# High halves of the transposed rows ahead of the low ones, one step of the first FFN pair later, token sums of the output parts some steps later

## The chip, the core and the metric

The kernel runs on one core of one Trainium2 chip. A core has a matrix engine (TensorE, in the profile PE, with its weight loads as PEld), two elementwise engines (VectorE = DVE and ScalarE = ACT), GpSimd (POOL), and queues for transfers between the chip's memory and the core (SyncE = SP issues most of them). The metric is the device time of one execution in microseconds; lower is better. Times in tables are medians of several runs. The profile comes from one further execution, with every instruction's start and duration.

## The reference

One layer of an encoder block, for 256 tokens of width 2048, all in float32. Three token mixers (dilated windows, grouped attention, attention to memory tokens) are merged by gates, projected and added to the input; then comes a gated feed-forward net (FFN) of inner width 5632. The change touches what stands from the projection on:

```python
merged = gates[:, :, 0] * (oa @ w_br_a) + gates[:, :, 1] * (ob @ w_br_b) + gates[:, :, 2] * (oc @ w_br_c)
x = x + merged @ w_o
hf = rms_norm(x, g_ffn) @ w_ffn_in
x = x + (silu(hf[..., :D_FF]) * hf[..., D_FF:]) @ w_ffn_out
```

## The kernel before

Every product of float32 matrices is made of three matmuls in a faster format (fp32r): each operand is split into a high half (the rounded value) and a low half (what is left), and high x high, high x low and low x high are summed in PSUM. ACT writes the high halves of a weight block (`whi`, in `halves`, line L397) and DVE the low ones (`wlo`, in `low`, L407). Both take from a ring of four buffers, and every fifth from a buffer of its own, so the `whi` of a step gets the buffer of the one five steps before, and must wait until PE has done that step's last matmul.

Work goes in pairs of output columns (`pair`), each 512 wide for 256 tokens in two halves (t = 0, 1); a pair runs a list of steps. A step reads weights, makes their halves and issues matmuls of a 128x128 stationary block against 512 columns:

- `dN`, `DN`: block N of the inner dimension, whole, for the first or the second column of the pair (12 matmuls each, into the sums Y, V or Z, Q).
- `fN`, `gN`, `hN`, `pN`, `qN`: block N by a scheme of seven products instead of eight (the scheme of Strassen and Winograd). `fN` needs both columns' weights (two loads and an adding load by POOL, in `fetch_both`), `gN` their sums (L506, L507, and L513 or L529 on DVE), `h`, `p` and `q` what is left of them. These steps also need sums of the token rows, which `token_sums` makes from a block of transposed rows: three subtractions on DVE (L796 to L798), then high halves on ACT (L130) and low ones on DVE (L131), named `forms` or `form` in the trace.

Matmuls and SP's transfers keep the order in which the program is written; the order of ACT's and DVE's other work is laid out by a scheduler at build time, by the order of the program and by priorities. Between steps, `tick` advances one of the waiting side jobs: such a job is a generator that yields the number of ticks until it wants to go on. In one tick at most one job is advanced, the earliest in the list first. Side jobs are:

- `later` of the projection (`projecting`): squares the new x (L878), transposes it on PE (`tp`), and writes x1T, the FFN's input, by `transposed`: for each of two halves of four 128-wide blocks, two blocks are scaled and split, block by block (ACT's high L133, DVE's low L134). Where a block is used for the seven products, ACT also copies it (`ffull`, L301) and `token_sums` follows.
- `later` of the FFN (`feeding`): multiplies silu(a) by b, transposes the result to hT, and for the last blocks of a group makes token sums in the same way.
- `sums_of`: adds the halves of one block of hT again and makes its token sums. It starts at the head of the output pairs.

The FFN's inner width is done in three groups (`feeding`); in each, pairs of `w_ffn` fill hT, then two output pairs with `w_ffn_out` add into x. The first FFN pair uses STEPS_FFN, the output pairs STEPS_OUT and STEPS_OUT2, in the last group STEPS_LAST and STEPS_LAST2. `run` prepares a step's halves four steps ahead of its matmuls.

## Time and profile before

| | us |
|---|---|
| three runs | 1368.82, 1368.85, 1505.42 |
| median | 1368.85 |
| profiled execution | 1369.74 |
| its span, first to last instruction | 1368.0 |
| mean granted clock of TensorE | 1.000 |

The busy times of the engines and the waits of PE stand in the prediction. Two more pieces of the page matter for reading it: the chain that ended last, followed back from the last instruction, by engine, and the costliest groups of ACT and DVE with the idle time before them.

```profile
PE 86%; DVE 8%; issue 2%; DMA 2%; ACT 1%; SPq 0%; DVEq 0%; ACTq 0%
...
L397 ACT ACTIVATE whi<-raw 128x1024 fp32r<-128x1024 f32 (+1 forms) x460 | 479.4, 1051 | 350.6 <-PE mmV L77 109.6
L407 DVE TENSOR_TENSOR wlo<-raw,whi 128x1024 fp32r<-128x1024 f32 (+1 forms) x460 | 546.8, 1210 | 80.7 <-ACT whi L397 77.5
```

A group's line gives line number, engine, operation, output and inputs, shape and count, then busy time and mean duration (ns), then the idle time of the engine before these instructions and what ended most of it. ACT's idle time before `whi` is ended by PE (a matmul that frees the buffer), DVE's before `wlo` by ACT. All matmuls have the line L77, that of the function which records them, so they are told apart by the names of their tiles: mmX, mmY, mmZ, mmV, mmW and mmQ are the sums of a pair.

### The profile page before, as it was taken

The numbers are of one execution on the slowest core, as the hardware profiler recorded it, in microseconds if no ns is written. First come the engines' busy times: TensorE is split into PE (matmuls) and PEld (weight loads), VectorE is DVE, ScalarE is ACT, GpSimd is POOL, SyncE is SP. The second block draws the span as 40 slices with busy tenths as digits, with TensorE's granted clock in tenths as the row PEclk, the third lists the DMA queues.
The fourth block names the chain that finished last, engine by engine and source line by source line (L and its number), as shares of the span: only waits on it lengthen the run. The fifth ranks groups of instructions, "written<-read, shape, count | busy, mean of one in ns | idle before, by whom it ended". The sixth has DMA issues, their size and how long they took to land.

```text
span 1368.0 us, 17866 instructions
## 1 busy us (share of the span) xinstructions
PE 1358.7 (99%) x6195; PEld 1125.7 (82%) x6195; DVE 1190.5 (87%) x1652; ACT 865.4 (63%) x1152; POOL 85.1 (6%) x97
## 2 busy tenths in 40 slices
PE   9999999999999999999999999999999999999998
PEld 7888888888888888887878888888888888888887
DVE  6868877759889888878999998989999989899998
ACT  7777665646665565656776666655666765566754
POOL 0010000000000100000000010000001000011000
PEclk9999999999999999999999999999999999999999
DMA  9976445557776775954777777777787767787673
GB/s 366 343 234 203 151 156 168 171 166 225 239 237 201 225 242 180 308 181 146 242 223 220 233 211 221 220 246 212 222 247 218 230 187 243 217 247 225 204 224 108
DMA packets 91674, 298.86 MB, mean 218 GB/s; under 512 B 10368, under 2 KB 12928, under 8 KB 91328
## 3 DMA queue, kind: packets, MB, share of 16 engines
q1 hardware_dynamic: 79488, 275.94, 60.2%
q0 software_dynamic: 11952, 21.76, 9.7%
q8 instruction: 48, 0.79, 0.2%
q14 instruction: 42, 0.34, 0.1%
q10 hardware_dynamic: 144, 0.02, 0.0%
HBM read 294.81 MB, written 2.88 MB: 218 GB/s over the span
## 4 chain that ended last, share of the span: by engine, by line
PE 86%; DVE 8%; issue 2%; DMA 2%; ACT 1%; SPq 0%; DVEq 0%; ACTq 0%
PE mm L77 16%; PE mmZ L77 14%; PE mmV L77 14%; PE mmY L77 14%; PE mmQ L77 11%; PE mmX L77 10%; DVE wlo L407 4%; PE mmW L77 3%; DMA raw<-in_w_ffn 2%; PE tp L77 1%; ACT whi L397 1%; PE sc L77 1%; PE o L77 1%; DVE t L506 1%; PE pT L77 1%
## 5 line engine op out<-in xcount | busy, mean ns | idle before, releaser
L397 ACT ACTIVATE whi<-raw 128x1024 fp32r<-128x1024 f32 (+1 forms) x460 | 479.4, 1051 | 350.6 <-PE mmV L77 109.6
L407 DVE TENSOR_TENSOR wlo<-raw,whi 128x1024 fp32r<-128x1024 f32 (+1 forms) x460 | 546.8, 1210 | 80.7 <-ACT whi L397 77.5
L77 PE MATMUL mm<-whi,xT 128*128 128x512 f32 x640 | 202.5, 393 | 0.0
L131 DVE TENSOR_TENSOR wlo<-raw,whi 128x1024 fp32r<-128x1024 f32 x82 | 102.1, 1248 | 43.6 <-ACT whi L130 42.9
L77 PEld LDWEIGHTS mm<-whi,xT 128*128 128x128 f32 x640 | 119.3, 188 | 23.5 <-issue 0.4
L130 ACT ACTIVATE whi<-raw 128x1024 fp32r<-128x1024 f32 x82 | 86.7, 1061 | 62.3 <-PE mm L77 45.4
L77 PE MATMUL mm<-wlo,xT 128*128 128x512 f32 x320 | 125.7, 393 | 0.0
L407 DVE TENSOR_TENSOR wlo<-t,whi 128x1024 fp32r<-128x1024 f32 x90 | 102.2, 1138 | 13.4 <-ACT whi L397 12.9
L397 ACT ACTIVATE whi<-t 128x1024 fp32r<-128x1024 f32 x90 | 89.0, 990 | 25.5 <-PE mmQ L77 11.4
L77 PE MATMUL mmX<-whi,forms 128*128 128x512 f32 x312 | 104.9, 389 | 0.0
L77 PE MATMUL mmY<-whi,x1T 128*128 128x512 f32 x266 | 96.7, 394 | 0.8 <-DVE x1T L134 0.8
L77 PE MATMUL mmV<-whi,x1T 128*128 128x512 f32 x266 | 91.3, 390 | 0.0
L77 PEld LDWEIGHTS mm<-wlo,xT 128*128 128x128 f32 x320 | 60.2, 188 | 12.3 <-issue 0.7
L77 PEld LDWEIGHTS mmX<-whi,forms 128*128 128x128 f32 x312 | 58.6, 188 | 12.3 <-ACT SB L448 0.2
L485 POOL DMA_DIRECT2D raw<-in_w_ffn x43 | 37.2, 865 | 441.0 <-DMA raw<-in_w_ffn 143.3
L77 PE MATMUL mmZ<-whi,x1T 128*128 128x512 f32 x180 | 63.0, 391 | 0.0
L77 PE MATMUL mmQ<-whi,x1T 128*128 128x512 f32 x180 | 62.8, 390 | 0.0
L77 PE MATMUL mmW<-whi,forms 128*128 128x512 f32 x156 | 61.6, 395 | 0.0
L77 PE MATMUL mmZ<-whi,forms 128*128 128x512 f32 x156 | 60.9, 390 | 0.0
L77 PE MATMUL mmX<-wlo,forms 128*128 128x512 f32 x156 | 60.8, 389 | 0.0
L77 PEld LDWEIGHTS mmY<-whi,x1T 128*128 128x128 f32 x266 | 50.0, 188 | 11.3 <-DVE x1T L134 1.2
L507 DVE TENSOR_TENSOR t<-t,raw 128x512 f32<-128x512 f32 x83 | 57.1, 688 | 1.6
(285 smaller groups left out, 2837.9 us busy)
## 6 DMA issues: line engine op xcount, KB each, us to landing
raw<-in_w_ffn SPq DMA_DIRECT2D x176, 512.0 KB, 4.7
raw<-in_w_gate SPq DMA_DIRECT2D x96, 512.0 KB, 4.4
raw<-in_w_ffn_out SPq DMA_DIRECT2D x88, 512.0 KB, 4.6
raw<-in_w_qkv SPq DMA_DIRECT2D x64, 512.0 KB, 4.3
raw<-in_w_o SPq DMA_DIRECT2D x32, 512.0 KB, 4.8
raw<-in_w_br SPq DMA_DIRECT2D x24, 512.0 KB, 4.2
raw<-in_w_ffn POOLq DMA_DIRECT2D x43, 256.0 KB, 5.5
raw<-in_w_mem SPq DMA_DIRECT2D x15, 512.0 KB, 8.3
```

Of the source, the lines that this page charges most:

```text
L77: ins = op(*args, **kw)
L130: nc.scalar.activation(hi, src, AF.Copy)
L131: nc.vector.tensor_sub(lo, src, hi.bitcast(F32))
L397: nc.follow(nc.scalar.activation(hi[:, o], v, AF.Copy))
L407: nc.follow(nc.vector.tensor_sub(*due.pop(0)))
L485: nc.gpsimd.dma_start(out=b2[:, 0], in_=src(u, 0)[:, :NC], accum_op=ALU.add)
L506: nc.follow(nc.vector.tensor_add(s2, b2[:, 0], b2[:, 1]))
L507: nc.follow(nc.vector.tensor_sub(s3, s2, b1[:, 0]))
```

## The change

Three edits:

1. In `transposed`, where gains are given (x1T), the high halves of both blocks are written on ACT first and the low halves of both after them on DVE (new lines L297 and L299), instead of high, low, high, low.
2. In STEPS_FFN, d5 and D5 each stand one step later, behind g2 and g3.
3. `sums_of` takes a number of ticks to wait before it begins: 3 for the output pairs of the first two FFN groups, 8 for the last. In `merging` and `projecting` it begins at once, as before.

```diff
-STEPS_FFN = "d0 D0 d1 D1 f2 f3 d5 g2 D5 g3 h2 f4 d6 g4 p0 p2 h4 D6 q0 q2 d7 D7".split()
+STEPS_FFN = "d0 D0 d1 D1 f2 f3 g2 d5 g3 D5 h2 f4 d6 g4 p0 p2 h4 D6 q0 q2 d7 D7".split()
...
             else:
+                d = [dst(2 * h + k, 1) for k in range(2)]
                 for k in range(2):
-                    d = dst(2 * h + k, 1)
-                    split(d[0], d[1], tp[:, k * S:(k + 1) * S], g(2 * h + k))
+                    nc.scalar.activation(d[k][0], tp[:, k * S:(k + 1) * S], AF.Copy, scale=g(2 * h + k))
+                for k in range(2):
+                    nc.vector.scalar_tensor_tensor(d[k][1], tp[:, k * S:(k + 1) * S], g(2 * h + k),
+                                                   d[k][0].bitcast(F32), op0=ALU.mult, op1=ALU.subtract)
...
-    def sums_of(lhs, these, room):
+    def sums_of(lhs, these, room, after=0):
 
         def steps():
+            if after:
+                yield after
             for u, to in zip(these, room):
...
-                sums_of(hTl, (1,), room[4:])
+                sums_of(hTl, (1,), room[4:], 8)
...
-                sums_of(hTl, (5,), room[4:])
+                sums_of(hTl, (5,), room[4:], 3)
```

From L301 on, the lines of the new file are three further down, from the token sums' end on five (`whi` L400, `wlo` L410, L506 is L509, L529 is L532).

How the instructions move, at three places. Names ending in a number are single buffers; a name of the same number is the same tile in both.

The first is DVE in the first `w_o` pair, where wlo_5980 is the low half of d4. Before:

```order
L796 TENSOR_TENSOR fraw_6009<-ffull_6006 128x256
L134 SCALAR_TENSOR_TENSOR x1T_5470<-tp_6033,gT_82,x1T_5470 128x256
L797 TENSOR_TENSOR fraw_6009<-fraw_6009,ffull_6006 128x128
L798 TENSOR_TENSOR fraw_6009<-fraw_6009,ffull_6006 128x128
L134 SCALAR_TENSOR_TENSOR x1T_5470<-tp_6033,gT_82,x1T_5470 128x256
L506 TENSOR_TENSOR t2_5853<-raw_5855 128x512
L507 TENSOR_TENSOR t3_5854<-t2_5853,raw2_5857 128x512
L407 TENSOR_TENSOR wlo_5980<-raw0_5977,whi_5979 128x1024
```

and after:

```order
L799 TENSOR_TENSOR fraw_6009<-ffull_6006 128x256
L800 TENSOR_TENSOR fraw_6009<-fraw_6009,ffull_6006 128x128
L801 TENSOR_TENSOR fraw_6009<-fraw_6009,ffull_6006 128x128
L509 TENSOR_TENSOR t2_5853<-raw_5855 128x512
L299 SCALAR_TENSOR_TENSOR x1T_5470<-tp_6033,gT_82,x1T_5470 128x256 x2
L510 TENSOR_TENSOR t3_5854<-t2_5853,raw2_5857 128x512
L410 TENSOR_TENSOR wlo_5980<-raw0_5977,whi_5979 128x1024
```

The low halves of x1T (tp_6033) now come as a pair, behind the token sums and L509. The same stretch on ACT, where whi_6053 is the next step's high half and ffull_6006 the copy that the token sums above read. Before:

```order
L397 ACTIVATE whi_6017<-raw_5855 128x1024
L133 ACTIVATE x1T_5471<-tp_5997,gT_82 128x256 x2
L397 ACTIVATE whi_6053<-raw5_6051 128x1024
L301 ACTIVATE ffull_6006<-tp_5997,gT_82 128x256 x2
L133 ACTIVATE x1T_5470<-tp_6033,gT_82 128x256 x2
```

and after:

```order
L400 ACTIVATE whi_6017<-raw_5855 128x1024
L297 ACTIVATE x1T_5471<-tp_5997,gT_82 128x256 x2
L304 ACTIVATE ffull_6006<-tp_5997,gT_82 128x256 x2
L400 ACTIVATE whi_6053<-raw5_6051 128x1024
L297 ACTIVATE x1T_5470<-tp_6033,gT_82 128x256 x2
```

The copy ffull_6006 has moved ahead of whi_6053.

The second place is DVE at the start of the first FFN pair; tp_6427 holds the transposed rows of the block that d5 reads. The low half of D5's weights is wlo_6471 before; after, wlo_6444 belongs to d5 and wlo_6471 to g3. Before:

```order
L407 TENSOR_TENSOR wlo_6471<-raw6_6468,whi_6470 128x1024
L529 TENSOR_TENSOR raw4_6256<-t2_6252,raw4_6256 128x512
L797 TENSOR_TENSOR fraw_6376<-fraw_6376,ffull_6373 128x128
L134 SCALAR_TENSOR_TENSOR x1T_5473<-tp_6454,gT_82,x1T_5473 128x256
L134 SCALAR_TENSOR_TENSOR x1T_5472<-tp_6427,gT_82,x1T_5472 128x256
```

and after:

```order
L299 SCALAR_TENSOR_TENSOR x1T_5472<-tp_6427,gT_82,x1T_5472 128x256 x2
L510 TENSOR_TENSOR t3_6253<-t2_6252,raw0_6279 128x512
L516 TENSOR_TENSOR raw4_6256<-t2_6252,raw0_6279 128x512
L410 TENSOR_TENSOR wlo_6444<-raw5_6441,whi_6443 128x1024
L147 SCALAR_TENSOR_TENSOR rs_y_6503<-rs_t_6502,rs_y_6498 128x2
L410 TENSOR_TENSOR wlo_6471<-raw2_6277,whi_6470 128x1024
```

The second low half of tp_6427, before behind wlo_6471 and three others, is now in a pair ahead of wlo_6444 and wlo_6471.

The third place is the first output pair of the first FFN group: forms_6251 written from fraw_7935 (before) or fraw_7955 (after) are the token forms of step g7; wlo_8040 belongs to p2, wlo_8057 to h5, wlo_8067 to q0. DVE before:

```order
L407 TENSOR_TENSOR wlo_8027<-t2_7744,whi_8026 128x1024
L529 TENSOR_TENSOR raw2_7748<-t2_7744,raw2_7748 128x512
L407 TENSOR_TENSOR wlo_8040<-t2_7744,whi_8039 128x512
L131 TENSOR_TENSOR forms_6251<-fraw_7935,forms_6251 128x512
L407 TENSOR_TENSOR wlo_8057<-raw2_7748,whi_8056 128x1024
L407 TENSOR_TENSOR wlo_8067<-t3_7745,whi_8066 128x1024
L529 TENSOR_TENSOR raw0_7963<-t2_7744,raw0_7963 128x512
```

and after:

```order
L532 TENSOR_TENSOR raw0_7739<-t2_7735,raw0_7739 128x512
L410 TENSOR_TENSOR wlo_8040<-t2_7735,whi_8039 128x512
L801 TENSOR_TENSOR fraw_7955<-fraw_7955,ffull_7952 128x128
L410 TENSOR_TENSOR wlo_8057<-raw0_7739,whi_8056 128x1024
L410 TENSOR_TENSOR wlo_8067<-t3_7736,whi_8066 128x1024
L532 TENSOR_TENSOR raw6_7963<-t2_7735,raw6_7963 128x512
L131 TENSOR_TENSOR forms_6251<-fraw_7955,forms_6251 128x512
```

The forms' low half now stands behind wlo_8057, wlo_8067 and the second L532. ACT at the same place, before:

```order
L397 ACTIVATE whi_8039<-t2_7744 128x512
L130 ACTIVATE forms_6251<-fraw_7935 128x512
L397 ACTIVATE whi_8056<-raw2_7748 128x1024
L397 ACTIVATE whi_8066<-t3_7745 128x1024
L448 ACTIVATE SB_8037<-mmW_8019 128x512
```

and after:

```order
L400 ACTIVATE whi_8039<-t2_7735 128x512
L400 ACTIVATE whi_8056<-raw0_7739 128x1024
L400 ACTIVATE whi_8066<-t3_7736 128x1024
L130 ACTIVATE forms_6251<-fraw_7955 128x512
L451 ACTIVATE SB_8037<-mmW_8019 128x512
```

The forms' high half has moved behind whi_8056 and whi_8066. The second FFN group has the same move in its first output pair.

## The prediction

> **What bounds the kernel now.** I read the page's busy times first, then the clock, then the waits of PE (times in us; the second list gives total, how often, longest).

> ```profile
> PE 1358.7 (99%) x6195; PEld 1125.7 (82%) x6195; DVE 1190.5 (87%) x1652; ACT 865.4 (63%) x1152; POOL 85.1 (6%) x97
> core 0: 1368.0 us, clock 1.000
> PE mmY L77 <- DVE wlo L407: 1.3, 2, 1.0
> PE mmZ L77 <- DVE wlo L407: 1.0, 3, 0.4
> PE mmY L77 <- DVE x1T L134: 0.8, 1, 0.8
> PE tp L77 <- DVE SA L924: 0.6, 1, 0.6
> ```

> TensorE is the bound: of the span it is idle for 1368.0 - 1358.7 = 9.3 us, at full clock. The change leaves the number of products as it is, so it can gain at most these 9.3 us (0.7%), by ending waits of PE, and it loses whatever new waits of PE it makes. So the question is place by place: which operand comes last when PE wants it. I went through the order of each engine before and after and looked up, for each place that moved, when PE wants the operand and when its maker could now be done. Four places matter. Since ACT is given a buffer for the next `whi` only when PE is through with an old one, ACT and DVE can't run far ahead, and a wait of PE is not made up later.

> **Place A, the first `w_o` pair (626 to 650 us).** The rows below are ACT, DVE and PE with start, duration, line, operation, and in brackets the idle time before and what ended it.

> ```profile
> 632.78 0.47 ACT L133 ACTIVATE x1T<-tp,gT 128x256 fp32r<-128x256 f32 x1 [0.55 <-DVE x1T L134]
> 634.02 1.06 ACT L397 ACTIVATE whi<-raw 128x1024 fp32r<-128x1024 f32 x1 [0.77 <-PE mmV L77]
> 634.99 0.82 ACT L301 ACTIVATE ffull<-tp,gT 128x256 f32<-128x256 f32 x2
> 635.84 0.42 DVE L796 TENSOR_TENSOR fraw<-ffull 128x256 f32<-128x256 f32 x1 [2.07 <-ACT ffull L301]
> 637.63 0.68 DVE L506 TENSOR_TENSOR t<-raw 128x512 f32<-128x512 f32 x1
> 638.96 4.62 DVE L407 TENSOR_TENSOR wlo<-raw,whi 128x1024 fp32r<-128x1024 f32 x4
> 638.56 0.63 PE L77 MATMUL mmY<-whi,mT 128*128 128x512 f32 x2
> 640.24 0.50 PE L77 MATMUL mmY<-wlo,mT 128*128 128x512 f32 x1 [1.04 <-DVE wlo L407]
> 640.57 0.62 PE L77 MATMUL mmY<-whi,mT 128*128 128x512 f32 x2
> ```

> The second matmul of the pair at 638.56 begins at 638.79, so PE wants d4's `wlo` at 639.01 and gets it at 640.24; the next start is 0.33 later instead of 0.227 (the step between matmuls that run freely, from the rows of place C: twelve in 2.72 us). That is 1.23 + 0.10 = 1.33 us. The cause is the 2.07 us in which DVE waited for `ffull`: ACT did it behind a `whi` that itself waited for PE until 634.02, and had lost 0.55 us because the second high half waited for the first low one. In the new order both high halves and `ffull` are ahead of that `whi`. ACT then does `ffull` at about 632.7, DVE its three subtractions by about 634.3 and L506 (new L509) as well, the last x1T pair of lows when ACT's highs are done (634.99 + 0.9 = 635.9, then 0.8 on DVE), L507 0.7, and d4's `wlo` starts at about 637.45, done at 637.45 + 1.22 = 638.7 against 639.01. **The 1.33 us go**, with 0.3 us to spare. Late next is d5's `wlo`, which by the same replay keeps about 0.3 us too. Both margins are small: the bounds of this term are -1.33 and 0.

> **Place B, start of the first FFN block (670 to 695 us).**

> ```profile
> 676.23 1.06 ACT L397 ACTIVATE whi<-raw 128x1024 fp32r<-128x1024 f32 x1 [0.55 <-ACT sq L878]
> 679.45 1.06 ACT L397 ACTIVATE whi<-raw 128x1024 fp32r<-128x1024 f32 x1 [1.43 <-issue]
> 684.82 1.22 DVE L407 TENSOR_TENSOR wlo<-raw,whi 128x1024 fp32r<-128x1024 f32 x1
> 686.76 0.87 DVE L134 SCALAR_TENSOR_TENSOR x1T<-tp,gT,x1T 128x256 fp32r<-128x256 f32 x2
> 686.51 0.39 PE L77 MATMUL mmY<-wlo,x1T 128*128 128x512 f32 x1
> 687.69 0.50 PE L77 MATMUL mmY<-whi,x1T 128*128 128x512 f32 x1 [0.79 <-DVE x1T L134]
> 688.02 0.40 PE L77 MATMUL mmV<-whi,x1T 128*128 128x512 f32 x1
> 670.00:695.00 25.00, 24.21 (x115) 19.69 (x114) 24.16 (x49) 16.78 (x27) 1.37 (x2) 1.00 0.58 177
> ```

> PE wants the low half of x1T at 686.51 + 0.227 = 686.74 and starts at 687.69; with the slow next step (0.33) that is 0.95 + 0.10 = 1.05 us. The low stands on DVE behind D5's `wlo`, L529 and L797. Now it stands ahead of d5's and g3's `wlo`, as a pair, and PE has g2's six matmuls (6 x 0.227 = 1.36 us) before d5. The later want alone is more than the wait. **The 1.05 us go.** Late next is D5's `wlo`, by the replay about 1.1 us early. The moved step d5 issues 24 matmuls, a `whi`, a `wlo` and one 512 KB load. On SP, f4's two loads now go ahead of d5's; POOL's adding load for f4 keeps its place among POOL's instructions. Two loads of 512 KB are 5.9 us at the 177 GB/s of this stretch (last number of the windows row, which gives the stretch, the busy time of PE, PE's weight loads, DVE, ACT and POOL, the granted clock, the DMA share and GB/s). d5's `whi` moves from the row 676.23 to about that of 679.45, so 3.2 us later. If the load had no slack before, up to 5.9 - 3.2 = 2.7 us could be lost; but ACT waited at 676.23 for its own `sq`, not for a transfer, and I count nothing. Bounds of place B: -1.05 and +1.65.

> **Place C, start of the output parts of FFN blocks 1 and 2 (twice).** Here the delay of the token sums works. Three steps later, they take the tick that before belonged to the last hT transposes, which move behind six and twelve matmuls. Behind those hang the last token forms: high half on ACT (L130), low on DVE (L131), which step g7 uses. The low half moves from behind p2's `wlo` to behind those of h5 and q0 and behind L529; the high half moves behind q0's `whi`. The rows of the first of the two places, then the second:

> ```profile
> 866.18 0.62 ACT L130 ACTIVATE forms<-fraw 128x512 fp32r<-128x512 f32 x1
> 868.37 0.68 DVE L131 TENSOR_TENSOR forms<-fraw,forms 128x512 fp32r<-128x512 f32 x1
> 869.67 1.06 ACT L397 ACTIVATE whi<-t 128x1024 fp32r<-128x1024 f32 x1 [0.31 <-PE mmZ L77]
> 870.64 0.58 ACT L448 ACTIVATE SB<-mmW 128x512 f32<-128x512 f32 x1
> 870.77 1.22 DVE L407 TENSOR_TENSOR wlo<-t,whi 128x1024 fp32r<-128x1024 f32 x1
> 871.91 0.68 DVE L529 TENSOR_TENSOR raw<-t,raw 128x512 f32<-128x512 f32 x1
> 872.51 0.69 DVE L407 TENSOR_TENSOR wlo<-t,whi 128x512 fp32r<-128x512 f32 x1
> 868.05 0.39 PE L77 MATMUL mmW<-whi,forms 128*128 128x512 f32 x1
> 869.41 0.39 PE L77 MATMUL mmW<-whi,forms 128*128 128x512 f32 x1
> 869.87 0.39 PE L77 MATMUL mmW<-whi,forms 128*128 128x512 f32 x1
> 870.77 0.39 PE L77 MATMUL mmX<-whi,form 128*128 128x512 f32 x1
> 1119.15 0.69 DVE L131 TENSOR_TENSOR forms<-fraw,forms 128x512 fp32r<-128x512 f32 x1
> 1120.45 1.06 ACT L397 ACTIVATE whi<-t 128x1024 fp32r<-128x1024 f32 x1 [0.31 <-PE mmZ L77]
> 1122.68 0.68 DVE L529 TENSOR_TENSOR raw<-t,raw 128x512 f32<-128x512 f32 x1
> ```

> PE does g6 from 868.05 and g7 from 869.41; g7's third matmul (869.87) is the first that uses the low half, which was done at 868.37 + 0.68 = 869.05, only 0.8 us ahead. q0's `whi` can't start before g6's last matmul, since it takes g6's buffer: the row 869.67 shows it released by PE's mmZ. Everything behind it now waits for PE to finish g6. ACT: the high half starts where SB's copy stood, 870.64, and ends at 871.26. So PE starts g7 at about 871.3 instead of 869.41. DVE: q0's `wlo` 870.77, L529 at 871.91, then in the slot of 872.51 the low half, done at 872.51 + 0.68 = 873.19; PE starts 0.06 later (as 687.69 follows 686.76 + 0.87), at 873.25. Lost: 873.25 - 869.87 = 3.38, and 0.10 for the slow step after, 3.48 us. At the second place the same rows lie at the same distances (`whi` 1120.45, forms 1119.15, L529 1122.68), so **+6.96 us in all**. After g7 everything is paced by PE as before. Bounds: 0, if the wait is hidden after all, and 2 x 3.48 as the upper end, since what stands ahead of the low half is counted to the last instruction.

> **Place D, the last block (sums eight steps later).**

> ```profile
> 1308.51 0.66 PE L77 MATMUL tp<-ident,SA 128*128 128x128 f32 x4 [0.59 <-DVE SA L924]
> ```

> This wait of 0.59 us is for the multiplication that makes SA; its place on DVE is unchanged, so it stays. The second transposes move behind g2 (1.36 us); their result is used by the pair's last steps. I count 0, with bounds of -0.6 and +0.6, the size of this wait.

> **The sum.** -1.33 - 1.05 + 6.96 + 0 = +4.58 us. The profiled execution took 1369.74 us with a span of 1368.0, 0.9 us above the median of 1368.85; it becomes 1374.3 (span 1372.6), and against the median 1368.85 + 4.58 = 1373.4.

> **The rivals.** *No wait at C* (the forms are ready in time, or the time is taken out of a later wait of PE): -2.38 alone, 1366.5, not slower than before. For it: before, the low half was 0.8 us early and the list at the head has, besides places A, B and D, no wait of PE over 0.4 us that could take the time up. Against: the two rows released by mmZ tie the chain to PE itself, so it can't start earlier. *A and B keep their waits* (the change doesn't do what it says there): their margins are 0.3 and 1.1 us, less than one `wlo` of 1.22. Then +6.96 alone, 1375.8; with one of them kept, 1374.5 to 1374.8. *The clock drops* at C and the time ends on the slower side. The row of place A and those after it show what a stall of 1.23 us does: one step of 0.33, then full speed, and the granted clock of that stretch and of the whole core is 1.000. C's 3.4 us are more than any wait of PE in this trace, but they come as two, of about 1.9 us (869.41 to 871.3) and 1.4 (the rest of 3.38, less the slow step), with two matmuls between. If PE then ran at half speed, every step of 0.227 would be 0.454 until the clock returned; it would have to stay low for 2 x (27.4 - 4.6) = 45.6 us in all to make the kernel 2% slower, and for about 3.4 us after each stall (as long again as the stall) it would cost 1.7 each: 1376.8. [...]

> **How the numbers follow.** The wait at C with the gains at A and B: 0.70, 1373.4, with a range of its own from 1371.8 to 1374.6 (D's bounds, and a part of A kept). No wait at C: 0.14, 1366.5. A or B kept: 0.10, 1374.5 to 1375.8. Clock: 0.04, of which 0.01 for a low clock that lasts beyond the 45.6 us. 0.02 is left for places I didn't see. The range reaches from 1366.0 to 1376.5: it takes in the largest rival below and the two waits kept above, and leaves out the clock and the unseen, 0.06. About 2% (27.4 us) is what a measurement of this kernel can tell from no change: faster by that is beyond the 9.3 us that PE is idle, 0.01; slower by that only by the lasting low clock or something unseen, 0.02; within it 0.97.

> **What would show it.** Of the changed kernel: at about 640 us no wait of PE for `wlo`, around 687 none for x1T. In the output parts of blocks 1 and 2, at about 867 and 1120 us, PE waits in mmW for ACT's forms (about 1.9 us) and then for DVE's forms (about 1.4), 3.4 us in all at each; the wait for SA near 1312 stays. PE's busy time changes by little, its idle time grows from 9.3 to about 14 us. Without the waits for forms the second term is wrong; with waits for `wlo` near 640 or `x1T` near 687 the first ones are.

## The result, and the profile after

| | before | changed |
|---|---|---|
| median of six runs each, us | 1368.84 | 1375.13 |
| lowest and highest of the changed kernel, us | | 1373.25 to 1376.37 |
| ratio to before, 95% interval | | 1.0051 (1.004 to 1.0061) |
| profiled execution, us | 1369.74 | 1375.19 |
| its span, us | 1368.0 | 1373.4 |

The changed kernel is slower, by 0.5%: clear of the noise of these runs, and within the 2% that the forecast calls no change. The forecast was 1373.4 with a range from 1366.0 to 1376.5. One of the six runs before took 1505.42 us, far from the others; the ratio leaves it out, so it is not the quotient of the two medians. The profile of the changed kernel: busy times, the clock, and the waits of PE, longest total first.

```profile
PE 1361.3 (99%) x6195; PEld 1126.7 (82%) x6195; DVE 1190.4 (87%) x1652; ACT 864.5 (63%) x1152; POOL 85.1 (6%) x97
core 0: 1373.4 us, clock 0.998
PE mmW L77 <- ACT forms L130: 3.5, 2, 1.7
PE mmW L77 <- DVE forms L131: 2.5, 2, 1.3
PE tp L77 <- DVE SA L929: 0.3, 1, 0.3
PE mmY L77 <- DVE wlo L410: 0.2, 1, 0.2
```

The waits of mmY for `wlo` (1.0) and for x1T (0.8) are gone; two waits for ACT's forms and two for DVE's have come. PE's idle time grew from 9.3 to 1373.4 - 1361.3 = 12.1 us. That is only 2.8 us of the 5.4 by which the span grew. The other 2.6 are in PE's busy time, with the same 6195 matmuls: some ran slower. The granted clock says where. Stretches of the changed kernel (from and to; busy time and count of PE, PE's weight loads, DVE, ACT, POOL; granted clock; DMA share, GB/s):

```profile
866.00:870.40 4.40, 1.41 (x6) 0.51 (x5) 3.94 (x6) 2.32 (x3) 0.00 (x0) 0.87 0.99 300
870.40:876.00 5.60, 5.60 (x13) 4.44 (x14) 0.92 (x2) 1.86 (x3) 0.00 (x0) 0.50 0.12 49
1122.00:1128.00 6.00, 3.01 (x13) 1.86 (x12) 4.47 (x7) 3.18 (x4) 0.00 (x0) 1.00 0.95 296
626.00:651.00 25.00, 25.00 (x120) 20.66 (x119) 21.45 (x35) 18.22 (x33) 0.00 (x0) 1.00 0.37 125
670.00:695.00 25.00, 25.00 (x119) 20.54 (x118) 24.91 (x46) 17.60 (x29) 0.86 (x1) 1.00 0.54 168
```

Places A and B are without any gap now (25.00 of 25.00). Behind the first of the two stalls at place C, PE ran at half clock for 5.6 us; behind the second it did not. The rows of the first stall, PE with start, duration and idle time before, then ACT and DVE:

```profile
866.28 0.39 PE L77 MATMUL mmZ<-whi,forms 128*128 128x512 f32 x1
868.39 0.50 PE L77 MATMUL mmW<-whi,forms 128*128 128x512 f32 x1 [1.73 <-ACT forms L130]
868.73 0.40 PE L77 MATMUL mmW<-wlo,forms 128*128 128x512 f32 x1
870.39 0.79 PE L77 MATMUL mmW<-whi,forms 128*128 128x512 f32 x1 [1.26 <-DVE forms L131]
870.98 0.63 PE L77 MATMUL mmZ<-whi,forms 128*128 128x512 f32 x1
871.41 0.63 PE L77 MATMUL mmZ<-wlo,forms 128*128 128x512 f32 x1
876.10 0.40 PE L77 MATMUL mmV<-whi,hT 128*128 128x512 f32 x1
...
866.77 1.06 ACT L400 ACTIVATE whi<-t 128x1024 fp32r<-128x1024 f32 x1
867.73 0.61 ACT L130 ACTIVATE forms<-fraw 128x512 fp32r<-128x512 f32 x1
867.92 1.22 DVE L410 TENSOR_TENSOR wlo<-t,whi 128x1024 fp32r<-128x1024 f32 x1
869.05 0.68 DVE L532 TENSOR_TENSOR raw<-t,raw 128x512 f32<-128x512 f32 x1
869.65 0.69 DVE L131 TENSOR_TENSOR forms<-fraw,forms 128x512 fp32r<-128x512 f32 x1
```

g6's last matmul starts at 866.28, so g7 was due at 866.51. It starts at 868.39, when ACT's high half is done (867.73 + 0.61), and its third matmul at 870.39, when DVE's low half is done (869.65 + 0.69). Then the steps are 0.43 us (870.98 to 871.41) instead of 0.227, up to 876.10.

### The profile page after: what moved, and what is told of

Same layout as the page of the kernel before. It is cut to its first block, busy times and chain, and to the rows that moved or that the text cites. A ratio compares the mean times of both kernels' runs of the same rounds, so it can differ in the third digit from the quotient of the medians.

```text
span 1373.4 us, 17875 instructions
## 1 busy us (share of the span) xinstructions
PE 1361.3 (99%) x6195; PEld 1126.7 (82%) x6195; DVE 1190.4 (87%) x1652; ACT 864.5 (63%) x1152; POOL 85.1 (6%) x97
## 4 chain that ended last, share of the span: by engine, by line
PE 90%; DVE 7%; issue 1%; DMA 1%; ACT 1%; SPq 0%; DVEq 0%; ACTq 0%
PE mm L77 16%; PE mmV L77 15%; PE mmY L77 15%; PE mmZ L77 15%; PE mmX L77 11%; PE mmQ L77 11%; DVE wlo L410 4%; PE mmW L77 4%; PE tp L77 1%; PE o L77 1%; PE sc L77 1%; DVE t L510 1%; ACT whi L400 1%; PE pT L77 1%; DVE t L509 0%
## 5 line engine op out<-in xcount | busy, mean ns | idle before, releaser
L400 ACT ACTIVATE whi<-raw 128x1024 fp32r<-128x1024 f32 (+1 forms) x460 | 478.9, 1051 | 348.0 <-PE mmV L77 108.7
L410 DVE TENSOR_TENSOR wlo<-raw,whi 128x1024 fp32r<-128x1024 f32 (+1 forms) x460 | 546.7, 1210 | 82.1 <-ACT whi L400 79.2
L77 PE MATMUL mm<-whi,xT 128*128 128x512 f32 x640 | 202.4, 393 | 0.0
L131 DVE TENSOR_TENSOR wlo<-raw,whi 128x1024 fp32r<-128x1024 f32 x82 | 102.1, 1248 | 43.6 <-ACT whi L130 42.4
L77 PEld LDWEIGHTS mm<-whi,xT 128*128 128x128 f32 x640 | 119.2, 188 | 23.5 <-issue 0.4
L130 ACT ACTIVATE whi<-raw 128x1024 fp32r<-128x1024 f32 x82 | 86.7, 1061 | 62.3 <-PE mm L77 45.5
L77 PE MATMUL mm<-wlo,xT 128*128 128x512 f32 x320 | 125.6, 393 | 0.0
L410 DVE TENSOR_TENSOR wlo<-t,whi 128x1024 fp32r<-128x1024 f32 x90 | 102.2, 1137 | 16.7 <-ACT whi L400 16.4
L77 PE MATMUL mmX<-whi,forms 128*128 128x512 f32 x312 | 105.7, 392 | 0.0
L400 ACT ACTIVATE whi<-t 128x1024 fp32r<-128x1024 f32 x90 | 88.9, 989 | 26.2 <-PE mmQ L77 12.3
L77 PE MATMUL mmY<-whi,x1T 128*128 128x512 f32 x266 | 96.7, 393 | 0.0
L77 PE MATMUL mmV<-whi,x1T 128*128 128x512 f32 x266 | 91.3, 390 | 0.0
L77 PEld LDWEIGHTS mm<-wlo,xT 128*128 128x128 f32 x320 | 60.1, 188 | 12.4 <-issue 0.7
L77 PEld LDWEIGHTS mmX<-whi,forms 128*128 128x128 f32 x312 | 59.1, 190 | 12.4
L77 PE MATMUL mmW<-whi,forms 128*128 128x512 f32 x156 | 62.1, 398 | 6.0 <-ACT forms L130 3.5
L77 PE MATMUL mmZ<-whi,x1T 128*128 128x512 f32 x180 | 62.9, 390 | 0.0
L77 PE MATMUL mmQ<-whi,x1T 128*128 128x512 f32 x180 | 62.8, 390 | 0.0
L77 PE MATMUL mmZ<-whi,forms 128*128 128x512 f32 x156 | 61.2, 392 | 0.0
L77 PE MATMUL mmX<-wlo,forms 128*128 128x512 f32 x156 | 61.2, 392 | 0.0
L77 PEld LDWEIGHTS mmV<-whi,x1T 128*128 128x128 f32 x266 | 49.9, 188 | 10.5
```

Of the source, the lines that this page charges most:

```text
L77: ins = op(*args, **kw)
L130: nc.scalar.activation(hi, src, AF.Copy)
L131: nc.vector.tensor_sub(lo, src, hi.bitcast(F32))
L400: nc.follow(nc.scalar.activation(hi[:, o], v, AF.Copy))
L410: nc.follow(nc.vector.tensor_sub(*due.pop(0)))
```

## The experiments

All kernels are timed beside the kernel before on the same chip, several runs each. The first four in this section were run together on one chip; then edit 1 alone, edit 2 alone, the eight ticks and the half filled wait; then the changed kernel again and the quarter filled wait. Differences in us are between medians; the ratios are worked out from all runs and can differ a little from the quotient of the medians. `A`, `B`, `C` and `D` are the places of the prediction.

**Edits 1 and 2 without the delays.**

```diff
-                sums_of(hTl, (1,), room[4:], 8)
+                sums_of(hTl, (1,), room[4:])
...
-                sums_of(hTl, (5,), room[4:], 3)
+                sums_of(hTl, (5,), room[4:])
```

> Edits 1 and 2 alone (high halves first; d5 and D5 a step later), all token sums at once as before. My account: the waits of places A (1.33 us) and B (1.05 us) are gone and nothing is added, so about 2.4 us less than before, granted clock 1.000. The rival in which A and B keep their waits: no difference to before. The rival in which the loss comes from one of these two edits: slower than before.

1365.57 us against 1368.53: ratio 0.9977 (0.9968 to 0.9985), 3.0 us less. The two edits are a gain, somewhat larger than the 2.4 us of the two waits.

**Edit 3 alone, in the first two groups.** The kernel before with `after` in `sums_of` and

```diff
-                sums_of(hTl, (5,), room[4:])
+                sums_of(hTl, (5,), room[4:], 3)
```

> Edit 3 alone in the first two FFN groups (sums three ticks later), everything else as before. My account: two waits for forms of about 3.5 us each, so 7 us more than before, and where the clock drops behind one of them (as it did at 870 us in the changed kernel's profile, about 3 us) up to 3 us more for each drop: 7 to 10 us in all, more than the 6.3 us of the whole change. The rival in which edits 1 and 2 take part in the loss: less than 6 us more than before.

1377.89 us against 1368.53: 1.0062 (1.005 to 1.0075), 9.4 us more by the medians and 8.5 by the ratio. All the loss is here. Waits and stretches of this kernel:

```profile
PE mmW L77 <- ACT forms L130: 3.5, 2, 1.7
PE mmW L77 <- DVE forms L131: 2.5, 2, 1.2
PE mmY L77 <- DVE wlo L407: 1.0, 1, 1.0
PE mmY L77 <- DVE x1T L134: 0.8, 1, 0.8
...
872.00:878.00 6.00, 5.87 (x26) 4.86 (x27) 3.07 (x5) 4.36 (x6) 0.00 (x0) 1.00 0.26 81
1122.00:1126.00 4.00, 1.03 (x4) 0.56 (x4) 3.56 (x4) 1.67 (x3) 0.00 (x0) 0.98 1.02 311
1126.00:1129.20 3.20, 3.20 (x8) 2.45 (x8) 0.69 (x1) 1.23 (x2) 0.00 (x0) 0.50 0.13 54
```

The waits at C are those of the changed kernel, the waits at A and B stand as before. In this profile the clock fell behind the second stall (0.50 from 1126.00) and not behind the first (1.00 from 872.00); in the first profile of the changed kernel it fell behind the first and not behind the second. The last section sets such stretches side by side.

**The wait filled with matmuls.** PE is kept busy while the forms are made:

```diff
                 def products():
+                    for _ in range(15 if order[0] == "d3" and u == 7 else 0):
+                        nc.tensor.matmul(ps["W"], lhsT=forms(6, 0)[0], rhs=hi[:, 0], start=False, stop=False)
                     mul("W", forms(u, 0), hi[:, 0], lo[:, 0])
```

> The changed kernel, with 15 matmuls more on PE ahead of g7 in the first output pair of the first two FFN groups. They add products that don't belong there to the sum W, so the output parts of these groups come out changed. They fill the wait: 15 times 0.227 is 3.41 us against a wait of 3.5, on PE alone. My account: the wait itself is replaced one for one, and only the clock's loss goes: granted clock 1.000 and no steps of 0.427 us behind g7; about 2.5 to 3 us less than the changed kernel, 4 us more than before. The rival in which the time above the forecast is not the clock's (transfers or a later wait): the same time as the changed kernel, or more.

1373.40 us against 1368.53: 1.0036 (1.0024 to 1.0049), 4.9 us more than before, where the whole change showed 6.3 and later 7.2. The two stretches in which the clock fell, in this kernel:

```profile
871.10:876.80 5.70, 5.70 (x26) 4.74 (x26) 2.90 (x4) 4.35 (x6) 0.00 (x0) 1.00 0.23 63
1120.00:1130.00 10.00, 10.00 (x45) 8.06 (x45) 6.67 (x10) 6.51 (x9) 0.00 (x0) 1.00 0.59 174
```

26 matmuls in the stretch in which the changed kernel got through 13. ACT's and DVE's chain is the same and takes as long; what is gone is the clock's part: 1.00 in both rows. The gain of 1.4 to 2.4 us is less than the 2.5 to 3 expected.

**Five ticks instead of three.**

```diff
-                sums_of(hTl, (5,), room[4:], 3)
+                sums_of(hTl, (5,), room[4:], 5)
```

> The changed kernel with the sums of the first two FFN groups five ticks later instead of three. The order then has the last token forms where they were before. My account: it is the tick that is taken, not the delay as such, that makes the waits; with five the waits for forms are gone, so 9 us less than the changed kernel where its clock drops, and 2.4 us less than before. The rival in which later sums cost by themselves: between before and the changed kernel.

1365.70 us: 0.9979 (0.997 to 0.9988), 2.8 us less than before. Later sums cost nothing by themselves; with three the sums' job takes the very tick in which the last hT transposes were due, with five it takes another. The traces show it on PE: the last two groups of hT transposes start 4.55 us apart before (848.06 and 852.61) and with five (845.15 and 849.70), and 5.93 with three (846.51 and 852.44), six matmuls more between them.

**Edit 1 alone** (the delays and the step list as before).

> Edit 1 alone. My account: it ends the wait of place A by itself (1.33 us), since the exchange between ACT and DVE is what kept the copy for the token sums late; place B's wait for x1T is shorter or gone too, because the low halves then come as pairs: 1.3 to 2.4 us less than before. The rival in which the step list does both: no difference to before.

1366.27 us against 1368.43: 0.9983 (0.9974 to 0.9991), 2.2 us less. Places A and B have no gap in it:

```profile
626.00:651.00 25.00, 25.00 (x120) 20.66 (x119) 21.45 (x34) 17.92 (x33) 0.00 (x0) 1.00 0.37 130
670.00:695.00 25.00, 25.00 (x119) 20.68 (x118) 24.77 (x45) 18.00 (x30) 0.94 (x2) 1.00 0.55 169
```

**Edit 2 alone** (STEPS_FFN with d5 and D5 a step later, the rest as before).

> Edit 2 alone. My account: place B's wait (1.05 us) is gone, place A's stays (1.33 us): 1 us less than before. The rival in which the second low half is still behind the other weights and is late at the later place too: no difference to before, with a wait of mmY for x1T.

1369.92 us against 1368.43: 1.0009 (1.0 to 1.0017). A miss: the gain of 1 us did not come; if anything there is a loss, since the interval begins at 1.0. PE and DVE around the place, then two stretches of this kernel:

```profile
684.20 0.39 PE L77 MATMUL mmY<-whi,x1T 128*128 128x512 f32 x1
686.43 0.47 PE L77 MATMUL mmW<-whi,forms 128*128 128x512 f32 x1 [1.84 <-DVE x1T L134]
685.21 0.68 DVE L529 TENSOR_TENSOR raw<-t,raw 128x512 f32<-128x512 f32 x1
685.81 0.86 DVE L134 SCALAR_TENSOR_TENSOR x1T<-tp,gT,x1T 128x256 fp32r<-128x256 f32 x2
...
683.00:687.40 4.40, 2.56 (x11) 1.80 (x11) 4.40 (x8) 2.71 (x4) 0.00 (x0) 1.00 0.47 139
687.40:690.80 3.40, 3.40 (x9) 2.65 (x8) 3.39 (x7) 1.60 (x3) 0.00 (x0) 0.50 0.88 267
```

g2's first matmul opens the sum mmW. Its operands are there; it waits for DVE's low half of x1T. The two have no value in common. In the code both mmW and the second transposed half take a PSUM bank of the same tag ("mm"), which has four banks, and the pair's sums V and Q hold two of them. So mmW can get a bank that DVE must first have read, and it opens 12 matmuls earlier now. That is read from the code and the wait; no run gave mmW another bank. The wait is 1.84 us instead of x1T's 0.79, and in this profile the clock is 0.50 from a microsecond behind it (the row from 687.40).

**The eight ticks alone.**

> The eight ticks in the last FFN group alone. My account: no effect that can be measured, the wait of tp for SA near 1308 us stays at 0.3 to 0.75 us; within 0.5 us of before. The rival in which it is the cause of the shorter wait for SA in the changed kernel: 0.3 to 0.5 us less, with that wait gone or shorter than 0.5 us.

1368.73 us against 1368.43: 1.0002 (0.9993 to 1.0011), no difference; the wait of tp for SA is 0.6 us as before.

**Half filled, quarter filled, and the changed kernel again.** As the filled wait, with 8 and with 4 matmuls in place of 15.

> As the filled wait, with 8 added matmuls instead of 15, so the sum W is changed in the same way. They fill 1.82 us, up to the moment when the high half of the forms is there; the wait for the low half (about 1.4 us) stays, alone. If a stall of 1.4 us with PE busy on both sides is too short to lower the clock: the same time as the filled wait within 0.5 us, granted clock 1.000 behind g7. If the last stall by itself is enough: steps of 0.427 us behind g7 in some runs and up to the changed kernel's time.

> As the filled wait, with 4 added matmuls (0.91 us, wrong terms in the sum W as there). Two stalls stay at each place, about 1.0 and 1.4 us with two matmuls between, 2.2 us of idle PE instead of 3.0. If what lowers the clock is the share of idle time within a few microseconds, a drop should be rarer than in the changed kernel: granted clock near 1.000 and about 4.5 to 5 us more than before. If any pair of stalls of over a microsecond lowers it: as the changed kernel.

> The changed kernel once more, on the same chip and beside the next one. My account: 6 to 7 us more than before; the granted clock of the runs below 1.000, and the runs differ by whether the clock drops at the first, the second or both output parts (3 us each). The rival in which the clock has no part: granted clock 1.000 and a spread no larger than that of before.

| kernel | idle time left at one place C, us | us | ratio to before (95%) | mean clock of its runs |
|---|---|---|---|---|
| changed, again | 1.7 + 1.3 | 1376.03 | 1.0054 (1.0041 to 1.0066) | 0.995, 0.998, 0.998, 0.999, 0.999 |
| quarter filled | 0.8 + 1.3 | 1372.80 | 1.0032 (1.0019 to 1.0044) | 1.000 in five, 0.999 in one |
| half filled | 1.2 | 1373.35 | 1.0035 (1.0022 to 1.0048) | 1.000 in four, 0.999 in one |
| filled | none | 1373.40 | 1.0036 (1.0024 to 1.0049) | 1.000 in four, 0.999 in one |

A mean clock of 0.999 turns up in runs of the kernel before too, so single runs are not to be read by it; the four kernels together are. The three filled ones agree within 0.6 us (4.0 to 4.9 us above the kernel before on their chips), with whatever part of the wait is filled; on the same chip the unfilled one is 3.2 us above the quarter filled. Half filled came out as expected; quarter filled, 4.0 us above before, and the repeat, 7.2 above, lie just outside the 4.5 to 5 and the 6 to 7 expected. In the profile of the repeat the clock fell at both places:

```profile
871.20:874.00 2.80, 2.80 (x7) 2.25 (x8) 0.10 (x1) 1.23 (x2) 0.00 (x0) 0.50 0.24 97
1126.90:1130.10 3.20, 3.20 (x8) 2.52 (x9) 0.53 (x1) 1.23 (x2) 0.00 (x0) 0.50 0.17 69
```

## Why the prediction was right, point by point

**Place A, right in size, cause and margin.** The wait is gone, and with it the 1.33 us. DVE and PE of the changed kernel:

```profile
636.89 2.35 DVE L410 TENSOR_TENSOR wlo<-raw,whi 128x1024 fp32r<-128x1024 f32 x2
638.44 0.39 PE L77 MATMUL mmY<-wlo,mT 128*128 128x512 f32 x1
```

The first of the two low halves is d4's: started at 636.89, ready 1.2 us later at 638.1, and used at 638.44, so 0.3 us early as forecast (the whole stretch lies 0.6 us earlier than in the profile before). Edit 1 alone does it.

**Place B, right in its sum, wrong in its reason.** The 1.05 us are gone. But "the later want alone is more than the wait" is not enough: the experiment with edit 2 alone shows that g2, moved ahead, meets a wait of its own for DVE's low half of x1T, most likely for a PSUM bank that the transposed rows still hold. I had followed the operands of the moved step and not its output. With edit 1 beside it that wait is gone too: the low halves come early. Edit 2 adds nothing that can be told: 1366.27 without it and 1365.57 with it, with intervals that overlap. The prediction's 24 matmuls are those of d5 and D5 together; d5 has 12. No term hangs on it.

**Place C, right.** Forecast 3.38 + 0.10 = 3.48 us each, in two waits of 1.9 and 1.4 us. Measured, from start to start less the free step of 0.227: 868.39 - 866.51 = 1.88 us for the high half, 0.11 for the slow step behind it, 870.39 - 868.73 - 0.227 = 1.43 for the low half, and 0.11 behind that: 3.53, 0.05 above the upper end of its bounds. The chain is tied to PE as forecast: q0's `whi` starts 0.49 us behind the start of g6's last matmul (866.28 to 866.77), 0.48 before (869.19 to 869.67). The row of DVE is the forecast row: `wlo`, L532, then the low half of the forms. The rival in which the wait does not come is out: its two waits stand in the profile, and the delay of three alone costs 8.5 to 9.4 us.

**Place D, right.** Nothing, by the eight ticks alone.

**The clock, the rival with 0.04, happened.** It was to cost 1.7 us behind each stall, with the clock low for about 3.4 us. Half speed for as long as the stall was the author's assumption, and no run shows it; the runs show a granted clock of 0.50 for 6.83 us at place C (869.26 to 876.08 in the first profile of the changed kernel) and, with edit 2 alone, for 3.41 us (687.38 to 690.79) behind a stall of 1.84. In time, the first profile has 876.10 - 870.39 = 5.71 us for 13 steps that take 13 x 0.227 = 2.95, less the slow step of 0.11: 2.65 us, at one of the two places. In the profile of the repeated run 7 and 8 matmuls stand in the rows at 0.50; at (876.10 - 870.98) / 12 - 0.227 = 0.20 us more for each, that is 1.4 and 1.6 us. What stood against this rival was that the stall comes in two, with two matmuls between. In the first profile the clock stayed at 1.00 behind such a pair at one of the two places and fell at the other; in the repeated run it fell at both. This is why the median is 1.7 us above the forecast; the filled kernels, which have C's loss without the clock's, lie at 1372.8 to 1373.4. That 1375.13 lies in the range is partly luck: it is above the 1371.8 to 1374.6 that the main account allowed, and the range reached further up for waits kept at A and B, which did not stay; it was said to leave the clock out.

**The sum.** Of the two profiles: C +7.1, clock +2.65, A -1.33, B -1.05, together +7.4; the span grew by 5.4. The remaining 2 us are short waits that stand in one profile and not in the other: two for weights near 948 and 1199 us (in the profile before 0.65 and 0.59 with their slow steps), the wait for SA, and some at the start. They are also why PE's idle time is 12.1 us and not the 14 of the forecast. They come and go between runs of the same code (the wait for weights near 951 us is 0.1 us in the first profile of the changed kernel and 0.5 in the second), so one profile against another is good to about 2 us in this kernel, and a term smaller than that needs its own experiment.

A version that beats both: edits 1 and 2 without the delays, or the whole change with a delay of five, 1365.6 and 1365.7 us, 0.2% under the kernel before. Edit 1 alone gives most of it.

## What to carry to other kernels

Side work that is moved by some steps takes the place of other side work, and it is that work's deadline which has to be looked up: here a delay of three ticks cost 9 us and a delay of five nothing. A step that is moved earlier needs its output's buffer as well as its operands, so look up who reads that buffer last; here that is the likely reason of the wait of 1.84 us, not a shown one. Here, with the matrix engine busy for 99% of the span, the stalls of place C (1.73 and 1.26 us) cost another 1.4 to 2.65 us through the clock where it fell, on top of C's 3.5. Filling the wait with other matmuls showed that part: the granted clock of its profile stayed at 1.00 there, and the kernel took 4.9 us more than before instead of 6.3 and 7.2.

## What was not expected of the hardware

```profile
865.85:869.26 3.41, 1.55 (x6) 0.65 (x4) 3.01 (x5) 2.47 (x3) 0.00 (x0) 1.00 0.97 303
869.26:872.67 3.41, 2.28 (x5) 1.82 (x6) 1.08 (x2) 0.70 (x2) 0.00 (x0) 0.50 0.56 184
872.67:876.08 3.41, 3.41 (x9) 2.64 (x8) 1.00 (x2) 1.15 (x2) 0.00 (x0) 0.50 0.00 0
1121.85:1125.26 3.41, 1.68 (x7) 1.07 (x7) 3.01 (x5) 2.64 (x3) 0.00 (x0) 1.00 0.99 326
1125.26:1128.67 3.41, 2.15 (x10) 1.44 (x9) 1.61 (x3) 1.05 (x2) 0.00 (x0) 1.00 0.75 217
...
683.96:687.37 3.41, 1.57 (x7) 1.03 (x6) 3.41 (x7) 1.76 (x3) 0.00 (x0) 1.00 0.61 178
687.38:690.79 3.41, 3.41 (x9) 2.65 (x9) 3.40 (x7) 1.62 (x3) 0.00 (x0) 0.50 0.88 267
```

Behind the first of these rows and behind that from 683.96, with PE busy for 1.55 and 1.57 us and so idle for 1.86 and 1.84, the clock fell. Behind the row from 1121.85, with 1.68 us busy, it did not, nor behind a stretch of the changed kernel with 1.66 (1367.61 to 1371.02; the clock is 1.00 from there to the end). It stayed at 0.50 behind the row with 2.28 and came back behind the two with 3.41. That would fit the two places of the changed kernel: at 866 us one stretch holds 1.86 us of the pair's idle time, at 1122 us a line of the grid divides it into 1.73 and 1.26. In the profile of the quarter filled kernel the first place has 4.40 - 2.32 = 2.08 us of idle time in two stalls, and the clock stayed at 1.00; how the grid divides them is not shown. It was 1.00 too behind the single stalls of 1.2 us (half filled) and 1.04 us (place A before). That the busy time in such a stretch decides is the author's reading of these few rows. They are from single profiles, and the busy time is the profile's, in which the ends of matmuls are modelled.
